# Hybrid encoder, FFN: first weights split beside the output projection's last tile, another order of the first products, down operands loaded beside the last products

## The chip, the cores and the metric

One core of one Trainium2 chip runs the whole forward pass in one launch. The metric is the device time of one execution in microseconds; the time of a kernel is the median of several runs.

## The reference, cut to what matters

Two layers over 1024 tokens of width 1024, float32 in and out. The mixer's output projection and the FFN are what the change is about:

```python
for i in range(DEPTH):                                    # DEPTH = 2
    y = mixer(x)                                          # ends in  mix @ w_out
    x = layer_norm(ALPHA * x + y, ln_mix_g[i], ln_mix_b[i])
    a, u = x @ w_gate[i], x @ w_up[i]                     # 1024 -> D_FF = 2816
    c = conv_b + sum(conv_w[j] * shifted(a, j - 1) for j in range(3))   # along the tokens
    f = (gelu(c) * u) @ w_down[i]
    x = layer_norm(ALPHA * x + f, ln_ffn_g[i], ln_ffn_b[i])
    x = x + sigmoid(x @ ple_w_gate[i]) * (p[i] @ ple_w_proj[i])
```

## The kernel before, in words

Every fp32 matrix product is made of three matmuls: an operand is split into a rounded part (h) and the rest (l), and h·h, h·l and l·h are summed in PSUM (`mm3`, lines 158 to 160). A split is a copy that rounds (on ACT by `nc.scalar.copy`, L324, or on POOL, L138) and a subtraction on DVE (`lo_part`, L141).

**Output projection** (`out_proj`, L1043 to L1077). Eight tiles of 128 tokens; each has two halves of 24 matmuls into a bank `po`, the residual addition (L1066), the LayerNorm (statistics on DVE, L869 and L872; the square root `rs` on POOL, L873 and L874; three instructions on a 128x1024 tile: `norm` L879 and times g L880 on DVE, plus b L881 on POOL, or on DVE for the last tile), the store `xmid` and, one tile later, `xt.put`: TensorE transposes the tile and the operand of the FFN is made of it.

**FFN products** (`ffn`, L1200 and on). Gate and up projections are worked in 22 blocks `m`, gate and up by turns. A block multiplies a 2 x 2 division of the weights with a 2 x 2 division of the tokens by seven products in place of eight. The weight operands are a00, a01, a11 and four sums, s1 = a10 + a11, s2 = s1 - a00, s4 = a01 - s2, s3 = a00 - a10 (`Weights`, L1079 and on; 128x512 each; tiles `wf` loaded, `ws` sums, `wh` and `wl` split parts). The token operands are made once per layer (`XSeven`, from L323): b00, b10, b11, t1 by `put`, and t2, t3, t4 in two halves by `finish` (L366 to L381), which needs the last tile: a half takes four additions on DVE or POOL (L318, 128x1024 each) and three splits. One product is 12 matmuls of 128x512. The results are summed in SBUF (`read`, L1134 to L1170): `m` copies a00 out of its bank, u = m + s2, and so on; the two banks `pa` hold a00 and s2 of a block, and the third block's a00 can't begin before the u addition of the first (L1142) has read them.

**Start.** The first two blocks (m = 0 and 1) are interleaved by hand, since the tokens' sums are still being made: a00 and a01 of both, then s1, s2, s3, a11, s4 of both. From block 2 on the order within a block is a00, s2, s3, s1, a01, a11, s4, and the next block's sums and splits are issued beside a block's products.

**Down projection** (`load` L1286, `down`). Gate times up goes to DRAM (`gated`, the spill L1198); then 22 pairs of tiles (128x1024 of `w_down` and of `gated`) are loaded as `dr`, split as `dh`, `dl` and multiplied two pairs at a time (bank `pd`); each token tile of the residual is `xn`, loaded from `xmid` (L1312).

The program is written as one stream. A framework works out the semaphores and a scheduler sets the order in each engine's queue, by its own estimate of times; each engine then works through its queue strictly in that order.

## Time and profile before

| | us |
|---|---|
| median of 3 runs | 3142.58 (3137.59 to 3142.8) |
| profiled execution | 3139.44 |
| its span, first to last instruction | 3137.6 |
| TensorE busy | 3023.3 (96% of the span) |
| VectorE, GpSimd busy | 2275.3, 1048.3 |
| mean granted TensorE clock | 0.987 |

The profiled execution took 3139.44 us, 3.1 us less than the median. The two layers have the same FFN; the stretch of layer 0 between 795 and 872 us (end of the output projection and first two blocks) recurs 1532.9 us later in layer 1, and the one at 1255 us (start of the down projection) recurs at 2788 us. Idle time in a view is put down to the engine, tile and line whose semaphore came last.

### The profile page before, as it was taken

The page shows a single profiled execution, that of the slowest core. Times are in us where ns is not written, and L with a number is a line of the kernel's source. Part 1 is how long each engine was busy: PE and PEld are TensorE (multiplying, and loading weights), DVE is VectorE, ACT ScalarE, POOL GpSimd, SP SyncE. Part 2 cuts the span into 40 slices and gives each one's busy share as a digit, 9 for nine tenths or more (in the row PEclk, how much of TensorE's full clock was granted, in tenths as well). Part 3 has the DMA queues.
Part 4 walks back from the last instruction along what each step waited for, and adds up shares of the span by engine and source line. Part 5 has one row for each costly group of instructions (what it writes and reads, how often), then busy time and mean ns, then how long its engine had stood idle before and what let it go on. Part 6 is the DMA issues. An engine that isn't in the chain of part 4 may idle for free.

```text
span 3137.6 us, 43123 instructions
## 1 busy us (share of the span) xinstructions
PE 3023.3 (96%) x15704; PEld 2590.5 (83%) x15704; DVE 2275.3 (73%) x3864; ACT 1182.2 (38%) x2502; POOL 1048.3 (33%) x1546
## 2 busy tenths in 40 slices
PE   8999999999799999999999999999888999999999
PEld 7888989888588888788889999998666888878887
DVE  6666487875887777766648777777679777767764
ACT  5555577761232222101225555555423222211111
POOL 4444534333422221101225555554333222201112
PEclk9999999999899999999999999999998999999999
DMA  3000100143122221623121100004322222244221
GB/s 119 28 28 25 31 28 8 36 131 124 67 81 81 86 84 67 226 101 108 54 68 31 35 28 28 28 18 134 103 99 68 81 81 81 81 167 141 101 74 67
DMA packets 89251, 237.52 MB, mean 76 GB/s; under 512 B 9040, under 2 KB 32720, under 8 KB 89040
## 3 DMA queue, kind: packets, MB, share of 16 engines
q1 hardware_dynamic: 89040, 234.76, 21.7%
q8 instruction: 125, 2.05, 0.3%
q14 instruction: 86, 0.70, 0.1%
HBM read 179.15 MB, written 55.57 MB: 75 GB/s over the span
## 4 chain that ended last, share of the span: by engine, by line
PE 82%; DVE 9%; DMA 3%; ACT 3%; issue 2%; POOL 2%; SPq 0%; DVEq 0%; ACTq 0%; POOLq 0%
PE pb L159 7%; PE pb L158 7%; PE pb L160 7%; PE xt L163 5%; PE pd L158 5%; PE pd L160 5%; PE pd L159 5%; PE pp L158 4%; PE pp L160 4%; PE pp L159 4%; PE s L582 3%; PE pa L158 3%; PE pa L160 2%; PE pa L159 2%; PE pg L158 2%
## 5 line engine op out<-in xcount | busy, mean ns | idle before, releaser
L158 PE MATMUL pd<-dh,dh 128*128 128x512 f32 x704 | 276.0, 392 | 8.5 <-ACT dh L324 7.5
L141 DVE TENSOR_TENSOR ptl<-xt,pth 128x512 fp32r<-128x512 f32 (+2 forms) x384 | 240.1, 652 | 57.8 <-ACT pth L397 41.3
L160 PE MATMUL pd<-dh,dl 128*128 128x512 f32 x704 | 275.1, 392 | 2.2 <-DVE dl L141 2.1
L1306 DVE TENSOR_TENSOR xn<-xn,pd 128x512 f32<-128x512 f32 x320 | 212.3, 684 | 88.5 <-PE pd L160 87.7
L159 PE MATMUL pd<-dl,dh 128*128 128x512 f32 x704 | 274.9, 391 | 0.0
L158 PE MATMUL pp<-wh,xth 128*128 128x384 f32 x768 | 266.4, 347 | 8.2 <-ACT wh L145 8.0
L159 PE MATMUL pp<-wl,xth 128*128 128x384 f32 x768 | 258.9, 337 | 1.3 <-DVE wl L148 1.3
L160 PE MATMUL pp<-wh,xtl 128*128 128x384 f32 x768 | 258.1, 336 | 0.0
L438 ACT ACTIVATE e<-s,nmx 128x1024 f32<-128x1024 f32 x192 | 214.4, 1118 | 96.6 <-DVE nmx L828 73.8
L158 PE MATMUL pb<-xt,wh 128*128 128x512 f32 x528 | 207.2, 392 | 0.0
L159 PE MATMUL pb<-xt,wh 128*128 128x512 f32 x528 | 206.9, 392 | 0.0
L160 PE MATMUL pb<-xt,wl 128*128 128x512 f32 x528 | 206.9, 392 | 0.0
L324 ACT CAST wh<-ws 128x512 fp32r<-128x512 f32 x132 | 81.7, 620 | 319.9 <-PE pb L159 261.8
L163 PE MATMUL xt<-ident,e 128*128 128x128 f32 x1440 | 194.7, 275 | 5.6 <-POOL e L731 3.0
L138 POOL TENSOR_SCALAR wh<-ws 128x512 fp32r<-128x512 f32 x44 | 29.8, 677 | 458.1 <-PE pa L159 428.8
L163 PEld LDWEIGHTS xt<-ident,e 128*128 128x128 f32 x1440 | 164.4, 141 | 18.7 <-POOL e L731 4.3
L141 DVE TENSOR_TENSOR wl<-ws,wh 128x512 fp32r<-128x512 f32 x176 | 160.8, 914 | 24.1 <-ACT wh L324 23.9
L324 ACT CAST dh<-dr 128x1024 fp32r<-128x1024 f32 x44 | 46.1, 1051 | 346.6 <-DMA dr<-gated 201.9
L138 POOL TENSOR_SCALAR dh<-dr 128x1024 fp32r<-128x1024 f32 x44 | 47.0, 1070 | 367.1 <-DMA dr<-in_w_down_dram 190.7
L158 PEld LDWEIGHTS pd<-dh,dh 128*128 128x128 f32 x704 | 132.9, 189 | 37.8 <-issue 8.3
L160 PEld LDWEIGHTS pd<-dh,dl 128*128 128x128 f32 x704 | 132.5, 188 | 32.9 <-DVE dl L141 5.3
L158 PEld LDWEIGHTS pp<-wh,xth 128*128 128x128 f32 x768 | 144.7, 189 | 13.8 <-ACT wh L145 8.9
(270 smaller groups left out, 8751.0 us busy)
## 6 DMA issues: line engine op xcount, KB each, us to landing
wf<-in_w_gate_dram SPq DMA_DIRECT2D x44, 512.0 KB, 3.2
wf<-in_w_up_dram SPq DMA_DIRECT2D x44, 512.0 KB, 4.2
gated<-c SPq DMA_DIRECT2D x44, 512.0 KB, 2.6
dr<-in_w_down_dram SPq DMA_DIRECT2D x44, 512.0 KB, 3.2
dr<-gated SPq DMA_DIRECT2D x44, 512.0 KB, 4.0
wr<-in_w_c_dram SPq DMA_DIRECT2D x32, 384.0 KB, 3.2
pes<-peo SPq DMA_DIRECT2D x64, 128.0 KB, 2.1
xmid<-xn SPq DMA_DIRECT2D x16, 512.0 KB, 2.9
```

Source lines behind the costliest of these rows:

```text
L138: nc.gpsimd.tensor_scalar(o, i, 1.0, 1.0, op0=ALU.mult, op1=ALU.mult)
L141: nc.vector.tensor_tensor(lo, src, f32(hi), op=ALU.subtract)
L158: nc.tensor.matmul(o, lhsT=lh, rhs=rh, start=start, stop=False)
L159: nc.tensor.matmul(o, lhsT=lh, rhs=rl, start=False, stop=False)
L160: nc.tensor.matmul(o, lhsT=ll, rhs=rh, start=False, stop=stop)
L163: nc.tensor.transpose(o, in_=i, identity=ident)
L324: nc.scalar.copy(h, v)
L438: nc.scalar.activation(dst, s, AF.Exp, bias=negmax, scale=1.0, accum_out=l)
L582: nc.tensor.matmul(s[:, kh * 512:kh * 512 + 512], lhsT=qt[:, hl, i, :], rhs=self.ks[kh][:, j, :], start=hl == 0, stop=hl == 1)
L1306: nc.vector.tensor_tensor(xns[t][:, sl], xns[t][:, sl], po, op=ALU.add)
```

## The change

It has three parts, the same in both layers.

1. In the output projection's last tile the weights of blocks 0 and 1 are loaded ahead of the products, and in the middle of its second half tile 6 is put and a00 and a01 of block 0 are split. The LayerNorm's last addition (plus b) of tile 6 is on DVE in place of POOL.
2. For blocks 0 and 1 all four weight sums are on POOL (s2 and s4 were on DVE), and so is the second addition of t4 in `finish`. `finish` is in two halves, whose t3 and t4 are split later. The order of the first products is a00, a01 of both blocks, then s1, s4, s2, s3, a11. The bank of s1 is freed by a copy on ACT; c00 has a tile of its own; of the additions that used the bank one is on POOL.
3. The down projection's first two pairs, the eight `xn` tiles and the next two pairs are loaded beside the seven products of the last block (`before_down`) and not behind them. To have room, the pool of split tiles stays as it was in the output projection.

On POOL, around the LayerNorm of tile 6 (`rs` ending in 10244, xn 10154) and of tile 7 (`rs` 10335 before, 10349 after), the order before was:

```order
L881 TENSOR_TENSOR xn_2415_10044<-xn_2415_10044,lngb_2353_9583 128x1024
L873 TENSOR_SCALAR rs_2448_10244<-mv_2447_10243 128x1
L874 TENSOR_TENSOR rs_2448_10244<-rs_2448_10244,mhalf_73 128x1
L881 TENSOR_TENSOR xn_2437_10154<-xn_2437_10154,lngb_2353_9583 128x1024
L318 TENSOR_TENSOR ws_2464_10358<-wf_2461_10351 128x512
L318 TENSOR_TENSOR ws_2466_10360<-wf_2460_10350,wf_2461_10351 128x512
L138 TENSOR_SCALAR wh_2470_10370<-wf_2460_10350 128x512
L873 TENSOR_SCALAR rs_2457_10335<-mv_2456_10334 128x1
L874 TENSOR_TENSOR rs_2457_10335<-rs_2457_10335,mhalf_73 128x1
L318 TENSOR_TENSOR ws_2472_10374<-wf_2463_10355 128x512
L318 TENSOR_TENSOR ws_2474_10376<-wf_2462_10354,wf_2463_10355 128x512
```

Tile 6's `rs` and plus b stood ahead of all sums. Now the same stretch of POOL reads (L874, L875 and L882 are the old L873, L874 and L881; names that begin with `w` are weights):

```order
L882 TENSOR_TENSOR xn_2415_10044<-xn_2415_10044,lngb_2353_9583 128x1024
L138 TENSOR_SCALAR w_2460_10331<-wf_2450_10256 128x512
L318 TENSOR_TENSOR ws_2464_10359<-wf_2451_10257 128x512
L318 TENSOR_TENSOR ws_2465_10360<-wf_2450_10256,wf_2451_10257 128x512
L874 TENSOR_SCALAR rs_2448_10244<-mv_2447_10243 128x1
L318 TENSOR_TENSOR ws_2464_10359<-ws_2464_10359,wf_2450_10256 128x512
L875 TENSOR_TENSOR rs_2448_10244<-rs_2448_10244,mhalf_73 128x1
L318 TENSOR_TENSOR ws_2465_10360<-wf_2450_10256,ws_2464_10359 128x512
L318 TENSOR_TENSOR ws_2468_10371<-wf_2453_10261 128x512
L318 TENSOR_TENSOR ws_2469_10372<-wf_2452_10260,wf_2453_10261 128x512
L318 TENSOR_TENSOR ws_2468_10371<-ws_2468_10371,wf_2452_10260 128x512
L318 TENSOR_TENSOR ws_2469_10372<-wf_2452_10260,ws_2468_10371 128x512
```

Eight sums now stand in a row around the second half of tile 6's `rs` and ahead of tile 7's, and tile 6's plus b is gone from here.

On DVE, up to the u addition of block 0 (`u` from `m` and `pa`; `xt2`, `xt3` and `xt4` are the token operands, `t3` and `t4` their sums), the rows before were:

```order
L141 TENSOR_TENSOR xt2_2503_10478<-t2_2430_10116,xt2_2502_10477 128x1024
L318 TENSOR_TENSOR t3_2508_10483<-t2_2430_10116,xb00_2370_9728 128x1024
L318 TENSOR_TENSOR t4_2509_10484<-xb10_2374_9732,t2_2430_10116 128x1024
L141 TENSOR_TENSOR wl_2526_10582<-wf_2463_10355,wh_2525_10581 128x512
L318 TENSOR_TENSOR t4_2509_10484<-t4_2509_10484,xb10_2376_9734 128x1024
L141 TENSOR_TENSOR wl_2529_10601<-ws_2467_10361,wh_2528_10600 128x512
L141 TENSOR_TENSOR wl_2531_10605<-ws_2475_10377,wh_2530_10604 128x512
L141 TENSOR_TENSOR xt4_2507_10482<-t4_2509_10484,xt4_2506_10481 128x1024
L141 TENSOR_TENSOR xt3_2505_10480<-t3_2508_10483,xt3_2504_10479 128x1024
L141 TENSOR_TENSOR wl_2537_10631<-wf_2514_10536,wh_2536_10630 128x512
L1142 TENSOR_TENSOR u_2527_10585<-m_2481_10403,pa_2480_10390 128x512
```

The second half's t4 and t3 splits were the last of the token operands. Now DVE has there:

```order
L141 TENSOR_TENSOR xt3_2484_10455<-c_2480_10451,xt3_2483_10454 128x1024
L141 TENSOR_TENSOR xt4_2486_10457<-c_2480_10451,xt4_2485_10456 128x1024
L141 TENSOR_TENSOR w_2505_10541<-ws_2469_10372,w_2505_10541 128x512
L141 TENSOR_TENSOR xt3_2499_10510<-t_2494_10505,xt3_2498_10509 128x1024
L141 TENSOR_TENSOR xt4_2501_10512<-t_2495_10506,xt4_2500_10511 128x1024
L141 TENSOR_TENSOR w_2508_10563<-wf_2451_10257,w_2508_10563 128x512
L141 TENSOR_TENSOR w_2509_10566<-wf_2453_10261,w_2509_10566 128x512
L141 TENSOR_TENSOR w_2527_10714<-wf_2510_10569,w_2527_10714 128x512
L141 TENSOR_TENSOR w_2520_10637<-wf_2510_10569,w_2520_10637 128x512
L318 TENSOR_TENSOR ws_2515_10602<-ws_2515_10602,wf_2510_10569 128x512
L318 TENSOR_TENSOR ws_2516_10603<-wf_2510_10569,ws_2515_10602 128x512
L1158 TENSOR_TENSOR u_2517_10608<-m_2471_10390,pa_2470_10377 128x512
```

The additions of t4's second term are gone from the row, the t3 and t4 splits of both halves stand together behind the t2 split, and the u addition still comes behind all of them.

On SP, at the end of layer 0's products (L1198 and L1236 are the spill of `gated`), the DMAs before were:

```order
L1198 DMA gated0_93<-c_2458_10345 128x1024
L1286 DMA dr_3110_13761<-in_w_down_dram 128x1024
L1286 DMA dr_3087_13715<-gated0_93 128x1024
L1198 DMA gated0_93<-c_2458_10345 128x1024
L1286 DMA dr_3113_13767<-gated0_93 128x1024
L1312 DMA xn_3090_13721<-xmid0_91 128x1024
...
L1286 DMA dr_3098_13737<-in_w_down_dram 128x1024
```

The `xn` loads followed the last spill. Now SP has there:

```order
L1236 DMA gated0_93<-c_2480_10451 128x1024 x2
L1273 DMA dr_2909_13438<-in_w_down_dram 128x1024
L1273 DMA dr_2912_13444<-gated0_93 128x1024
L1273 DMA dr_2949_13596<-in_w_down_dram 128x1024
L1273 DMA dr_2916_13464<-in_w_down_dram 128x1024
L1273 DMA dr_2919_13470<-gated0_93 128x1024
L1273 DMA dr_2952_13602<-gated0_93 128x1024
L1286 DMA xn_2924_13491<-xmid0_91 128x1024
...
L1273 DMA dr_2935_13537<-in_w_down_dram 128x1024
L1236 DMA gated0_93<-c_2480_10451 128x1024 x2
L1273 DMA dr_2938_13543<-gated0_93 128x1024
```

The four loads of the first two pairs and all eight `xn` loads now stand ahead of the last block's two spills; before, one of the four stood between the two spills and the eight behind both.

The diff, cut to its core:

```diff
-        def finish(self):
...
-            for j in range(2):
...
-                split_value(t2, h["t2"], l["t2"])
-                add(t3, t2, h["b00"], ALU.subtract)
-                add(t4, h["b10"], t2, ALU.subtract)
-                add(t3, t3, l["b00"], ALU.subtract, nc.gpsimd)
-                add(t4, t4, l["b10"])
+        def finish(self, j, temps):
+
...
+            t2, (t3, t4) = self.t2[j], temps
+            add(t3, t2, h["b00"], ALU.subtract)
+            add(t3, t3, l["b00"], ALU.subtract, nc.gpsimd)
+            add(t4, h["b10"], t2, ALU.subtract)
+            add(t4, t4, l["b10"], ALU.add, nc.gpsimd)
+            split_value(t2, h["t2"], l["t2"])
+            self.t2[j] = None
+
+            def step():
+                split_value(t3, h["t3"], l["t3"])
                 split_value(t4, h["t4"], l["t4"])
-                split_value(t3, h["t3"], l["t3"])
-            self.t2 = None
+            return step
 
...
-        def linear(t):
+        def linear(t, beside):
             mh, ml = m.pop(t)
...
                 for k in range(NK):
+                    if n == 1 and k == NK // 2:
+                        beside()
                     mm3(po, mh[:, k, :], ml[:, k, :], w[k][0][:, sl], w[k][1][:, sl], k == 0, k == NK - 1)
...
@@ -1069,10 +1072,18 @@
         for t in range(NT):
             residual(t)
             load(t + 1)
-            linear(t)
-            if t:
-                xt.put(t - 1, xns[t - 1])
-            ln(xns[t], t == NT - 1)
+            if t == NT - 1:
+                early(0)
+
+                def beside():
+                    xt.put(t - 1, xns[t - 1])
+                    early(1)
+                linear(t, beside)
+            else:
+                linear(t, lambda: None)
+                if t:
+                    xt.put(t - 1, xns[t - 1])
+            ln(xns[t], t >= NT - 2)
             nc.sync.dma_start(out=xmid[i][t], in_=xns[t])
...
-        def steps(self, make=None):
...
-                add(s3, a00, a10, ALU.subtract, nc.gpsimd)
-                add(s2, s1, a00, ALU.subtract)
-                add(s4, a01, s2, ALU.subtract)
...
+        def sums(self, eng=None):
+            (a00, a01), (a10, a11) = ((r[:, 0:4, :], r[:, 4:8, :]) for r in self.r)
+            s12, s34 = (unit("ws", [P, 2, 4, P]) for _ in range(2))
+            s1, s2, s3, s4 = s12[:, 0], s12[:, 1], s34[:, 0], s34[:, 1]
+            add(s1, a10, a11, ALU.add, nc.gpsimd)
+            add(s2, s1, a00, ALU.subtract, eng)
+            add(s4, a01, s2, ALU.subtract, eng)
+            add(s3, a00, a10, ALU.subtract, nc.gpsimd)
+            self.v.update({"a11": a11, "s1": s1, "s2": s2, "s3": s3, "s4": s4})
+
...
+        def go_ahead(self, c00):
+
+            self.ahead, self.c00 = True, c00
+            self.sums.insert(0, ("k5", ("s1",)))
...
+                elif name == "k5":
+                    self.c11 = mid2("c11", [P, 512])
+                    nc.scalar.copy(self.c11, self.o["s1"])
+                elif name == "c11" and self.ahead:
+                    nc.gpsimd.tensor_tensor(self.u2, self.u2, self.c11, op=ALU.add)
+                    nc.vector.tensor_tensor(self.c11, self.u3, self.c11, op=ALU.add)
...
+    def ffn_early(w):
+        def early(n):
+            if n == 0:
+                w[0].load()
+                w[1].load()
+            else:
+                w[0].split("a00")
+                w[0].split("a01")
+        return early
...
-        new_region(2)
-        w[0].load()
-        w[1].load()
...
-        order = [(0, "a00"), (0, "a01"), (1, "a00"), (1, "a01"), (0, "s1"), (1, "s1"), (0, "s2"), (1, "s2"), (0, "s3"), (1, "s3"),
-                 (0, "a11"), (1, "a11"), (0, "s4"), (1, "s4")]
...
-            if n == 1:
-                late()
-                for q in ("s1", "s2"):
-                    for a in range(2):
-                        steps[a][n2[q]]()
-                xt.finish()
-            if n == 4:
-                w[2].load()
-                w[3].load()
-            if n in (5, 6, 7):
...
+        def before_down(j):
+
+            if j in (0, 1):
+                load(j)
+            if j in (2, 3):
+                for t in range(4 * (j - 2), 4 * (j - 2) + 4):
+                    xns.append(unit("xn", [P, 1024]))
+                    nc.sync.dma_start(out=xns[t], in_=xmid[i][t])
+            if j in (4, 5):
+                load(j - 2)
+
+
+        pr = [Products(w[m], xt) for m in range(NF)]
+        order = [(0, "a00"), (0, "a01"), (1, "a00"), (1, "a01")]
+        order += [(m, name) for name in ("s1", "s4", "s2", "s3", "a11") for m in range(2)]
+        order += [(m, name) for m in range(2, NF) for name in Products.ORDER]
+        w[0].sums(nc.gpsimd)
+        w[1].split("a00", False)
+        w[1].split("a01", False)
+        w[1].sums(nc.gpsimd)
...
+            if n == 1:
+                c00 = unit("c00", [P, 2, 512])
+                for a in range(2):
+                    pr[a].go_ahead(c00[:, a])
+                w[0].split("s1")
+                w[1].split("s1")
+            if n == 2:
+                late()
+                new_c()
+                c2 = late_c[0]
+                first[0] = xt.finish(0, [c2[:, a, :].rearrange("p (k q) -> p k q", k=2) for a in range(2)])
+            if n == 3:
+                w[0].split("s4")
+                w[1].split("s4")
+                w[0].split("s2", True)
+                w[1].split("s2", True)
+            if n == 4:
+                first[1] = xt.finish(1, [unit("t", [P, 2, 512]) for _ in range(2)])
+            if n == 5:
+                w[0].split("s3")
+                first[0]()
+                w[1].split("s3")
+                first[1]()
+            if n == 6:
+                w[0].split("a11")
+                w[1].split("a11")
+                w[2].load()
+            if n == 7:
+                w[3].load()
+                todo = w[2].steps()
+            for _ in range({8: 1, 10: 2, 11: 1, 12: 1, 13: 3}.get(n, 0)):
+                todo.pop(0)()
...
+            if m == NF - 1:
+                before_down(Products.ORDER.index(name))
+        finished(len(order) - 1)
...
-        load(0)
-        load(1)
-        for t in range(NT):
-            xns.append(unit("xn", [P, 1024]))
-            nc.sync.dma_start(out=xns[t], in_=xmid[i][t])
-        load(2)
-        load(3)
         yield xns
```

## Rows read from the trace of the kernel before

**Rows 1.** Part 1 of the page: busy time of TensorE (PE), its weight loads, VectorE (DVE), ScalarE (ACT) and GpSimd (POOL), with the share of the span and the number of instructions.

```profile
PE 3023.3 (96%) x15704; PEld 2590.5 (83%) x15704; DVE 2275.3 (73%) x3864; ACT 1182.2 (38%) x2502; POOL 1048.3 (33%) x1546
```

**Rows 2.** The windows view, busy microseconds of each engine in a stretch with the number of instructions that began in it, then PEclk (the granted TensorE clock as a share of 2.4 GHz), the DMA share and GB/s. The first stretch lies in the middle of layer 0's products; the next two are the start of the products in layer 0 and in layer 1; the last two are slices of the start in layer 0.

```profile
1000.00:1200.00 200.00, 200.00 (x875) 163.03 (x874) 157.19 (x231) 59.79 (x86) 50.40 (x51) 1.00 0.24 85
801.00:872.00 71.00, 52.66 (x200) 40.88 (x199) 67.12 (x88) 22.92 (x36) 28.36 (x21) 0.81 0.15 52
2334.00:2405.00 71.00, 52.38 (x200) 40.66 (x198) 67.29 (x88) 23.14 (x37) 28.31 (x21) 0.81 0.15 52
835.00:850.00 15.00, 6.12 (x13) 4.08 (x14) 15.00 (x15) 3.70 (x6) 7.15 (x3) 0.61 0.31 105
850.00:865.00 15.00, 15.00 (x56) 12.01 (x56) 11.76 (x19) 3.98 (x6) 4.29 (x5) 0.82 0.01 1
```

**Rows 3.** The view of waits on PE between 780 and 880 us (layer 0's start): who waited, for which engine, tile and line, then microseconds in total, number of times, longest.

```profile
PE pa L158 <- DVE u L1142: 7.5, 1, 7.5
PE pa L158 <- ACT wh L324: 4.6, 1, 4.6
PE pa L158 <- ACT xt L324: 3.3, 1, 3.3
PE pa L160 <- DVE wl L141: 1.6, 1, 1.6
```

**Rows 4.** The same view of PE over the whole run.

```profile
PE pa L158 <- DVE u L1142: 15.2, 2, 7.7
...
PE pd L158 <- ACT dh L324: 7.5, 2, 3.9
```

**Rows 5.** The timeline of DVE in layer 0's start: begin, duration, line, operation, output tile and inputs, shapes.

```profile
794.87 0.21 DVE L872 BATCH_NORM_AGGREGATE mv<-st 128x2 f32<-128x12 f32 x1
...
822.25 0.68 DVE L141 TENSOR_TENSOR wl<-ws,wh 128x512 fp32r<-128x512 f32 x1
...
824.23 1.23 DVE L141 TENSOR_TENSOR xt<-t,xt 128x1024 fp32r<-128x1024 f32 x1
825.38 1.22 DVE L318 TENSOR_TENSOR t<-t,xb 128x1024 f32<-128x1024 f32 x1
826.51 1.22 DVE L318 TENSOR_TENSOR t<-xb,t 128x1024 f32<-128x1024 f32 x1
827.65 2.88 DVE L141 TENSOR_TENSOR wl<-ws,wh 128x512 fp32r<-128x512 f32 x1
...
839.71 2.86 DVE L141 TENSOR_TENSOR wl<-wf,wh 128x512 fp32r<-128x512 f32 x1
...
848.77 1.27 DVE L1142 TENSOR_TENSOR u<-m,pa 128x512 f32<-128x512 f32 x2
```

**Rows 6.** The timeline of POOL in the same stretch.

```profile
795.16 0.19 POOL L873 TENSOR_SCALAR rs<-mv 128x1 f32<-128x1 f32 x1 [6.22 <-DVE mv L872]
...
798.36 2.39 POOL L881 TENSOR_TENSOR xn<-xn,lngb 128x1024 f32<-128x1024 f32 x1 [2.37 <-DVE xn L880]
801.10 1.28 POOL L318 TENSOR_TENSOR ws<-wf 128x512 f32<-128x512 f32 x1 [0.34 <-PE po L160]
...
823.08 0.62 POOL L138 TENSOR_SCALAR wh<-ws 128x512 fp32r<-128x512 f32 x1 [8.83 <-DVE wl L141]
826.68 3.30 POOL L318 TENSOR_TENSOR t<-t,xb 128x1024 f32<-128x1024 f32 x1 [2.98 <-DVE t L318]
...
838.74 3.29 POOL L318 TENSOR_TENSOR t<-t,xb 128x1024 f32<-128x1024 f32 x1 [5.16 <-DVE t L318]
```

**Rows 7.** The groups of POOL instructions by line and shape between 794.9 and 848.8 us: count, busy microseconds, mean ns of one, idle time before them and its releaser.

```profile
L318 POOL TENSOR_TENSOR t<-t,xb 128x1024 f32<-128x1024 f32 x2 | 6.6, 3296 | 8.1 <-DVE t L318 8.1
L318 POOL TENSOR_TENSOR ws<-wf,wf 128x512 f32<-128x512 f32 x3 | 5.0, 1660 | 0.0
...
L138 POOL TENSOR_SCALAR wh<-wf 128x512 fp32r<-128x512 f32 x4 | 4.4, 1118 | 0.0
```

**Rows 8.** The windows view again: the first 45 us of the down projection in layer 0, the 45 us behind them, and the first 45 us in layer 1.

```profile
1255.00:1300.00 45.00, 39.35 (x162) 30.71 (x161) 30.96 (x38) 5.19 (x6) 5.22 (x5) 0.96 0.70 266
1300.00:1345.00 45.00, 45.00 (x200) 37.26 (x200) 36.77 (x48) 7.33 (x7) 6.33 (x6) 1.00 0.47 164
2787.70:2832.70 45.00, 39.95 (x163) 30.91 (x162) 30.54 (x39) 5.47 (x6) 5.24 (x5) 0.96 0.70 267
```

**Rows 9.** The view of waits on PE between 1255 and 1300 us.

```profile
PE pd L158 <- ACT dh L324: 3.9, 1, 3.9
PE pd L160 <- DVE dl L141: 1.3, 1, 1.3
```

**Rows 10.** The timeline of SP's DMA queue at the end of layer 0's products (the time is that of the issue).

```profile
1229.69 0.32 SPq L1286 DMA_DIRECT2D dr<-gated  x1
1237.02 0.33 SPq L1286 DMA_DIRECT2D dr<-in_w_down_dram  x1
...
1255.22 0.33 SPq L1286 DMA_DIRECT2D dr<-in_w_down_dram  x1
1255.60 0.45 SPq L1286 DMA_DIRECT2D dr<-gated  x1
```

**Rows 11.** The timeline of ACT there.

```profile
1241.75 1.03 ACT L324 CAST dh<-dr 128x1024 fp32r<-128x1024 f32 x1
1260.54 1.04 ACT L324 CAST dh<-dr 128x1024 fp32r<-128x1024 f32 x1 [17.77 <-DMA dr<-gated]
```

More of the change, by code (lines that the diff above doesn't have):

```diff
@@ L1163, in read @@
                 elif name == "c00":
-                    plus(self.m, self.m, "a01")
-                    self.c00 = self.m
+                    if self.c00 is None:
+                        self.c00 = self.m
+                    plus(self.c00, self.m, "a01")
                 elif name == "c10":
```

116 lines of the change are left out of this document (45 added, 71 removed).

## Prediction

> **What bounds the kernel now.** I read the page's busy times first: TensorE is busy 96% of the span, the other engines are far below [rows 1]. The windows say where the last 4% are: in the middle of the products PE has 875 matmuls in 200 us and no idle time, which is 0.2286 us for each [rows 2]. So nothing in the steady blocks can be gained, and what the change does there (other buffers, the same instructions) I put at nothing: PE covers it, and DVE has 43 us of slack in 200. The places that the change touches are two in each layer. At the start of the products 200 matmuls begin in 71 us [rows 2] where 71/0.2286 = 310 would fit: 25 us are lost per layer. In the first 45 us of the down projection 162 begin where the next 45 us hold 200: 38 x 0.225 = 8.6 us lost, and 37 x 0.225 = 8.3 in layer 1 [rows 8]. Together 67 us are the most that both layers could give back. The view of waits names them: at the start 7.5 us for the u addition on DVE, 4.6 and 3.3 for casts on ACT, 1.6 for a split on DVE [rows 3], in both layers alike (15.2 us, two times [rows 4]); at the down projection 3.9 for a cast of a loaded operand and 1.3 for its split [rows 9]. Behind the u addition stands DVE: between 835 and 850 us it is busy for 15.00 of 15.00 us while PE has 6.12 [rows 2]. So the start is a question of DVE's queue up to that addition, not of PE.
>
> **What holds DVE.** Its prices: 0.60 us from start to start for a 128x512 instruction in SBUF (duration 0.68), 1.14 for 128x1024 (824.23, 825.38, 826.51) [rows 5]. POOL's: 1.28 for a 128x512 sum, 2.39 for a 128x1024 addition, 0.62 for a copy [rows 6]. But the 128x512 split that costs 0.68 alone took 2.88 and 2.86 while POOL did an addition of 128x1024, and that addition took 3.30 and 3.29 in place of 2.39 [rows 5, 6]. The split ends at 827.65 + 2.88 = 830.53, POOL's addition at 829.98; the other pair at 842.57 and 842.03. So DVE waited for POOL to the end and then worked its own 0.55 us, and POOL had waited for the DVE instruction before it. The Trainium skill, page "SBUF — State Buffer", section "Who interferes with whom", has this as a rule: of a DVE instruction with two SBUF inputs and a GpSimd one that reads SBUF the later is blocked until the first is done; the trace agrees in these four rows. I take from the rows that work in SBUF on the two engines adds up, save where DVE reads PSUM or is idle.
>
> **The start, step by step.** From tile 6's aggregate (794.87) to the end of the two u additions (848.77 + 1.2) [rows 5] are 55.0 us of DVE. By the order these are 19 instructions of 128x512 (11.4 us), 15 of 128x1024 (17.1), 20 of 128x256 at 0.33 (6.6), two norms, the statistics and a residual addition (4.0): 39.1 of its own. In the same time POOL has five sums (6.4), three 128x1024 additions (7.2) and six copies (about 4): 17.8. Stepping both queues in their order, the later of two SBUF instructions waiting for the other, DVE is held for 12.2 us and idle for 3.8, and the u addition comes at 850.2, within 1 us of the trace; without the holding it would be 13 us too early. That is why I trust the stepping for the new order, estimate as it is.
> The change takes four sums and one t4 addition for each half off DVE, and gives it tile 6's plus b, two c00 additions and an earlier split: 16 of 128x512 and 14 of 128x1024, 36.7 us in all. POOL gets nine sums, four 128x1024 additions and eight copies: 26.2. DVE gains 2.4 and is held for 20.7 in place of 12.2, with 4.4 idle: 61.8 us, 6.8 more. It also begins later: tile 6's `rs`, which POOL did at 795.16, straight after the aggregate [rows 6], stands behind two sums and is cut by a third, and plus b follows on DVE; the tile, whose plus b ended at 800.75, is ready at about 806.8, and the row starts 1.9 us later. The u addition so comes 8.7 us later, at 858.2 us. The Trainium skill, page "Perfetto Trace Analysis", section "Optimizing Scalar/DVE Operations", says that offloading between these two engines "might not help", as they share a port; on this part it speaks against the change. By the rows it is so here: DVE loses 8.5 - 2.4 = 6.1 us net by the move. (Where it were not so, the sum would be that of rival 1.)
> What pays is the order of the products. Before, PE could do 8 of the 14 first products (a00, a01, s1, s2) ahead of the u addition, now 12 (s4 and s3 too): 4 x 12 x 0.2268 = 10.9 us of matmuls are moved into the wait. PE's own gaps in the new order: it begins a00 at 807.7 in place of 806.5, a gap of 6.3 us ahead of s2's second half, which needs t2 of the second half, and 4.3 us ahead of the third block. Net 10.9 - 8.7 = 2.2, and with less of it at the lower granted clock (0.61 and 0.82 in the slices before [rows 2]) 3.1 us. In layer 1 another sum stands ahead of the power in `rs`, and the same steps give 1.7. Bounds per layer: with POOL's additions 1.25 times as long the start gives back up to 5 us less than that, so about -2; without any holding it gives 9 us more.
> The early split of a00 and a01 of block 0 takes the 4.6 us wait for ACT's cast [rows 3] away, but only in name: tile 6's transposes, which stand in front of these products on PE, are now late themselves, by 6 us. The copy of s1's bank on ACT is free, ACT is busy 22.92 of 71 us [rows 2]; POOL's one addition on u falls behind the critical point.
>
> **The down projection.** The second pair's `dr` was issued at 1255.22 and 1255.60, when PE had begun the first pair, and ACT cast it at 1260.54 after 17.77 us of waiting for the DMA; the first pair had been loaded at 1229.69 and 1237.02 and cast at 1241.75 [rows 10, 11]. The scheduler thus had half of the gain already. Now both pairs and the `xn` loads are ahead of the last two spills, beside the seven products of the last block (84 x 0.2268 = 19 us). The 3.9 and the 1.3 go [rows 9], and most of the slow matmuls that follow them (0.96 granted [rows 8]). What is late next is DVE: the pairs' splits are four of 128x1024 (4.6 us) in the last block, and the casts of the second group behind it; I leave 0.6 us of waiting at the second group. Stepped through, the stretch from the first `pd` takes 44.2 in place of 50.4 us: 6.2 per layer, with 5.2 (the two waits alone) and 8.6 as bounds. The new spill and loads on SP stall nobody: the spill waits behind loads whose buffers are free by then, and its data are needed in the last group.
>
> **Sum.** Layer 0: 3.1 + 6.2 = 9.3; layer 1: 1.7 + 6.2 = 7.9; together 17 us off 3139.4, so 3122 by the profiled execution, which stands 3.1 under the median: 3125.
>
> **Rivals.** (1) POOL's extra work doesn't hold DVE, since it falls where DVE waits anyway: then only DVE's shorter queue counts, and the same steps give 18.6 and 13.5 us per layer with the down part, 32 in all: 3110. For it: POOL is busy only 28.36 of 71 us [rows 2]. Against it: the four stretched rows, and 12.2 us of holding without which the old order can't be had.
> (2) POOL becomes the bound of the start, and the kernel slower. The place is POOL's queue from tile 6's `rs` to the last t4 addition, where eight sums stand ahead of tile 7's `rs` and four 128x1024 additions ahead of the splits. If each of its instructions costs what it cost beside a busy DVE, 1.66, 3.30 and 1.12 [rows 7], it has 9 x 1.66 + 4 x 3.30 + 8 x 1.12 = 37.1 us, and if none of it overlaps DVE's 36.7 the row takes 73.8: the u addition comes 20.7 us later, not 8.7, and each start loses 9.6 us where 2.4 was won on average. With 12.4 from the down parts that is 6.8 us slower: 3149. It decides from a delay of about 20 us; between 15 and 20 it eats just what the down part gives, about 3140. Against it: for the old order this sum gives 39.1 + 8.3 + 9.9 + 6.7 = 64 where the trace has 55.0.
> (3) The down loads gain nothing, because the waits only move to the splits on DVE or to the second group: then only the start's 4.8 are left, 3138, no change to be measured. Against it: DVE is busy 157 of 200 us in the blocks [rows 2], so there is room for 4.6 us.
>
> **How the numbers follow.** Forecast 0.55 (3115 to 3134: gains of 9 to 25 us, from POOL 1.25 times dearer to half of the holding gone); rival 1 0.20; rival 2 slower 0.10, eating the gain 0.08; rival 3 0.07. A measurement of this kernel can tell 0.2%, 6.3 us, from no change. Faster by more than that 0.75, within it 0.15, slower 0.10. The range goes from 3107 (rival 1 with 3 us to spare) to 3139 (rival 3 within), and leaves out about 0.2: rival 2 whole, and a little past rival 1.
>
> **What would show it.** Right: PE's wait for the u addition at the third block shrinks from 7.5 to about 4, a new wait of some 6 us at s2 for the t2 operand appears; tile 6's transposes begin at about 807; DVE still has no idle time between 835 and 850; the wait for `dh` at the down projection (7.5 us in two [rows 4]) is gone, and the first 45 us there hold some 190 matmuls. Rival 1: no wait at the third block, and 128x512 splits near 0.7 us beside POOL's additions. Rival 2: POOL busy throughout the start, PE waiting for token operands t3 or t4 for over 10 us. Wrong altogether: a wait in the steady blocks (fewer than 875 matmuls in 200 us), which I put at nothing.

## The result

The changed kernel takes 3123.38 us (median of 4 runs, 3122.67 to 3124.18), the kernel before 3141.32 (4 runs): a ratio of 0.995, 95% interval 0.9937 to 0.9962. The profiled execution spans 3120.8 us where that of before spanned 3137.6, 16.8 us less. Page part 1 of the changed kernel:

```profile
PE 3014.5 (97%) x15704; PEld 2589.3 (83%) x15704; DVE 2295.5 (74%) x3850; ACT 1184.5 (38%) x2506; POOL 1084.9 (35%) x1560
```

Against [rows 1] PE has the same 15704 instructions and is busy 9 us less; DVE is busy 20 us longer and POOL 37, though DVE has 14 instructions fewer and POOL 14 more. Both helpers work longer, and the kernel is faster all the same.

To see where, I take the time at which the same matmul begins in both traces, counting matmuls. "Start" goes from the output projection's last tile (the 337th `po` matmul of layer 0; in layer 1 the 317th, 20 earlier, which makes both numbers there 5.8 us longer) to the 1001st matmul of the layer's products; "blocks" from there to the last product matmul; "down" from there to the 601st `pd` matmul.

| us | before | changed | difference | predicted |
|---|---|---|---|---|
| start, layer 0 | 270.74 | 267.62 | -3.1 | -3.1 |
| start, layer 1 | 276.41 | 275.85 | -0.6 | -1.7 |
| blocks, both layers | 388.33 | 387.78 | -0.6 | 0 |
| down, layer 0 | 144.82 | 137.87 | -6.95 | -6.2 |
| down, layer 1 | 144.52 | 137.58 | -6.94 | -6.2 |
| all else (unchanged code) | 1912.7 | 1914.1 | +1.4 | 0 |

The last line isn't put down to the change: in the traces of all the runs below, the stretch between the layers alone varies between 917.4 and 922.6 us with the same code. Kernels with the same start differ too: the changed kernel, e2_start_only and e9_region below by up to 0.5 us in layer 0 and 0.9 in layer 1. So the 0.6 us of layer 1 can't be told from nothing.

The windows of the changed kernel (busy microseconds with counts, then granted clock, DMA share, GB/s):

```profile
801.00:872.00 71.00, 55.26 (x218) 44.18 (x219) 69.42 (x78) 22.52 (x35) 44.10 (x26) 0.88 0.13 45
...
835.00:850.00 15.00, 10.51 (x42) 7.76 (x41) 15.00 (x9) 4.94 (x6) 12.11 (x6) 0.94 0.30 103
1000.00:1200.00 200.00, 200.00 (x875) 162.96 (x874) 163.06 (x232) 60.12 (x87) 52.87 (x50) 1.00 0.23 82
1251.20:1296.20 45.00, 43.81 (x193) 35.68 (x192) 34.75 (x44) 6.21 (x6) 6.28 (x6) 1.00 0.67 237
2777.10:2822.10 45.00, 43.98 (x195) 36.03 (x194) 34.80 (x45) 6.22 (x6) 6.29 (x6) 1.00 0.68 240
```

At the start 218 matmuls begin in 71 us where 200 did, and in the slice from 835 to 850 us 42 where 13 did [rows 2]; DVE is busy for 15.00 of 15.00 us in it as before, and POOL for 12.11 where it was 7.15. The middle of the blocks has its 875 matmuls in 200 us still. The first 45 us of the down projection hold 193 and 195, not 162 and 163 [rows 8].

PE's waits at the start of layer 0, to set beside [rows 3]:

```profile
PE xt L163 <- DVE xn L882: 8.5, 2, 6.1
PE pb L159 <- DVE xt L141: 3.8, 1, 3.8
PE pa L158 <- DVE u L1158: 3.1, 1, 3.1
...
PE pa L159 <- DVE xt L141: 0.7, 1, 0.7
```

and two of layer 1:

```profile
PE xt L163 <- DVE xn L882: 10.9, 2, 5.5
PE pa L158 <- DVE u L1158: 4.4, 1, 4.4
```

The 7.5 us for the u addition have become 3.1 and 4.4. In place of the 4.6 for ACT's cast PE now waits for tile 6's and tile 7's LayerNorm, 8.5 and 10.9 us in two waits, and the second half of a token operand has a wait of 3.8 (it is s3's, `pb`, not s2's). DVE's timeline (begin, duration), to set beside [rows 5]:

```profile
800.51 1.74 DVE L880 TENSOR_SCALAR xn<-xn,mv,rs 128x1024 f32<-128x1024 f32 x1 [4.15 <-POOL rs L875]
...
804.49 2.17 DVE L882 TENSOR_TENSOR xn<-xn,lngb 128x1024 f32<-128x1024 f32 x1
...
835.38 3.41 DVE L141 TENSOR_TENSOR xt<-t,xt 128x1024 fp32r<-128x1024 f32 x1
...
839.73 6.75 DVE L141 TENSOR_TENSOR xt<-c,xt 128x1024 fp32r<-128x1024 f32 x2
...
856.42 1.28 DVE L1158 TENSOR_TENSOR u<-m,pa 128x512 f32<-128x512 f32 x2
```

and POOL's, to set beside [rows 6]:

```profile
799.92 0.55 POOL L875 TENSOR_TENSOR rs<-rs,mhalf 128x1 f32<-128x1 f32 x1
...
825.80 4.66 POOL L138 TENSOR_SCALAR w<-ws 128x512 fp32r<-128x512 f32 x1 [6.64 <-PE pb L160]
...
831.00 6.70 POOL L318 TENSOR_TENSOR c<-c,xb 128x1024 f32<-128x1024 f32 x2
...
839.24 6.16 POOL L318 TENSOR_TENSOR t<-t,xb 128x1024 f32<-128x1024 f32 x2
```

Tile 6's `rs`, whose power ends at 800.47, is done 4.3 us behind the beginning of the aggregate (796.16); before, it was done 1.1 us behind it (at 795.99). DVE stands idle for 4.15 us until then; the norm takes 1.74 and plus b 2.17, beside POOL's sums. Of the token operands' splits of 128x1024 one costs 3.41 and two cost 6.75, where one alone costs 1.14, while POOL does its additions. The u addition begins at 856.42, that is 66.9 us behind the beginning of this stretch (789.52); before, 58.9 behind it (848.77 and 789.84), so it is 8.0 us later. In layer 1 it is 9.7 later (68.6 us behind the beginning, 58.9 before).

### The profile page after: what moved, and what is told of

Its sections match the earlier page's. It is cut to its first block, busy times and chain, and to the rows that moved or that the text cites. A ratio compares the mean times of both kernels' runs of the same rounds, so it can differ in the third digit from the quotient of the medians.

```text
span 3120.8 us, 43023 instructions
## 1 busy us (share of the span) xinstructions
PE 3014.5 (97%) x15704; PEld 2589.3 (83%) x15704; DVE 2295.5 (74%) x3850; ACT 1184.5 (38%) x2506; POOL 1084.9 (35%) x1560
## 4 chain that ended last, share of the span: by engine, by line
PE 60%; DVE 5%; DMA 2%; POOL 2%; issue 1%; ACT 1%; SPq 0%; DVEq 0%; ACTq 0%; POOLq 0%
PE pb L160 5%; PE pb L159 5%; PE pb L158 5%; PE pd L158 5%; PE pd L159 5%; PE pd L160 5%; PE s L583 4%; PE pp L159 3%; PE pp L160 3%; PE pp L158 3%; PE pa L158 2%; PE xt L163 2%; PE pa L160 2%; PE pa L159 2%; PE pg L158 2%; PE pg L160 2%
## 5 line engine op out<-in xcount | busy, mean ns | idle before, releaser
L324 ACT CAST w<-ws 128x512 fp32r<-128x512 f32 x132 | 81.5, 621 | 355.7 <-PE pb L160 284.1
L159 PE MATMUL pb<-xt,w 128*128 128x512 f32 x528 | 207.2, 392 | 7.2 <-DVE xt L141 7.2
L158 PE MATMUL pb<-xt,w 128*128 128x512 f32 x528 | 206.8, 392 | 0.0
L160 PE MATMUL pb<-xt,w 128*128 128x512 f32 x528 | 206.4, 391 | 0.0
L138 POOL TENSOR_SCALAR w<-ws 128x512 fp32r<-128x512 f32 x44 | 34.9, 794 | 426.5 <-PE pa L160 403.2
L141 DVE TENSOR_TENSOR w<-ws,w 128x512 fp32r<-128x512 f32 x176 | 160.5, 914 | 1.5 <-ACT w L324 0.5
L160 PEld LDWEIGHTS pd<-dh,dl 128*128 128x128 f32 x704 | 132.1, 188 | 27.6
```

The costliest lines, as they stand in the source:

```text
L138: nc.gpsimd.tensor_scalar(o, i, 1.0, 1.0, op0=ALU.mult, op1=ALU.mult)
L141: nc.vector.tensor_tensor(lo, src, f32(hi), op=ALU.subtract)
L158: nc.tensor.matmul(o, lhsT=lh, rhs=rh, start=start, stop=False)
L159: nc.tensor.matmul(o, lhsT=lh, rhs=rl, start=False, stop=False)
L160: nc.tensor.matmul(o, lhsT=ll, rhs=rh, start=False, stop=stop)
L324: nc.scalar.copy(h, v)
```

## Experiments

Ten kernels ran; each is judged by its time and by the stretches of the table above, read in its trace. Ratios go by the kernel before as it ran beside each: 3138.93 us with e1 to e5, 3140.99 with e6 to e9, 3140.08 with e10 and e11.

| us | start 0 | start 1 | blocks 0 | down 0 | down 1 | median |
|---|---|---|---|---|---|---|
| before | 270.74 | 276.41 | 194.17 | 144.82 | 144.52 | 3138.9 to 3141.3 |
| changed | 267.62 | 275.85 | 193.86 | 137.87 | 137.58 | 3123.38 |
| e1_down_only | 270.60 | 275.97 | 194.77 | 136.23 | 136.23 | 3122.68 |
| e2_start_only | 268.09 | 276.71 | 194.11 | 142.34 | 142.22 | 3133.54 |
| e4_t4_dve | 266.15 | 274.57 | 193.89 | 138.73 | 138.09 | 3121.15 |
| e5_no_pool | 259.67 | 264.21 | 193.91 | 138.95 | 138.86 | 3103.87 |
| e6_old_order | 271.93 | 281.04 | 193.89 | 139.58 | 137.32 | 3131.40 |
| e7_before_no_pool | 267.61 | 273.99 | 194.25 | 145.28 | 145.34 | 3133.39 |
| e8_ahead | 256.56 | 263.02 | 193.89 | 138.78 | 137.22 | 3101.95 |
| e9_region | 268.09 | 276.04 | 194.68 | 137.00 | 137.02 | 3125.45 |
| e10_copies_act | 265.59 | 272.77 | 193.91 | 138.35 | 137.43 | 3119.84 |
| e11_sums_dve | 269.92 | 275.57 | 193.88 | 138.87 | 139.04 | 3126.30 |

**The parts apart.** The down part alone, put on the kernel before (`before_down` and `load` as in the change, ahead of the product loop):

```diff
+            if m == NF - 1:
+                before_down(Products.ORDER.index(name))
         finished(len(order) - 1)
...
-        load(0)
-        load(1)
...
         yield xns
```

> The kernel before with part 3 alone: the first two pairs, the xn tiles and the next two pairs of the down projection are loaded beside the last block's seven products; the start of the products is as before. Theory (the two parts are independent, and the down part is the larger): the stretch from the last product to the 200th matmul of the down projection loses 6.9 us per layer, as in the changed kernel, so about 13.9 us in all, 3127.5 where the kernel before has 3141.3; the start keeps its 7.5 us wait for the u addition. Rival (the down part needs the room that the changed start leaves in the buffers, or lives on the changed pool of split tiles): under 7 us in all, 3135 or more.

Measured 3122.68 us (3121.37 to 3124.27), ratio 0.9948, interval 0.9936 to 0.9961: as much as the whole change within the intervals, so parts 1 and 2 add nothing to part 3 that the time shows. The start is as before, with a wait of 7.7 us for the u addition. The down stretch loses 8.6 and 8.3 us, more than the 6.9 expected and all of the loss that the windows had shown, and the blocks ahead of it are 0.6 us longer. The window of its first 45 us is as full as any:

```profile
1252.90:1297.90 45.00, 45.00 (x201) 37.24 (x200) 36.39 (x47) 6.27 (x7) 6.57 (x6) 1.00 0.56 197
```

The changed kernel with this part undone:

```diff
-            if m == NF - 1:
-                before_down(Products.ORDER.index(name))
         finished(len(order) - 1)
+        for j in range(6):
+            before_down(j)
```

> The changed kernel with part 3 undone: the down operands and xn tiles are issued behind the last product again. Theory: only the start's gain is left, 3.4 us in layer 0 and 0.6 in layer 1 by the trace of the changed kernel, about 4 in all: 3137, no change that can be measured; the down projection has its wait of some 3.9 us for a cast of dh again. Rival (the start alone is worth the larger part, by the page's 0.995): 3130 or less.

Measured 3133.54 us (3130.28 to 3136.43), ratio 0.9982, interval 0.9973 to 0.9991: 5.4 us, between the theory and the rival, of which the starts have 2.6 and -0.3 and the down stretches 2.5 and 2.3. PE's waits at the down projection there:

```profile
PE pd L158 <- ACT dh L324: 2.1, 1, 2.1
PE pd L160 <- DVE dl L141: 0.7, 2, 0.6
```

The wait for `dh` is 2.1, not 3.9 [rows 9], with the loads behind the last product again. So a third of the changed kernel's down gain comes from elsewhere than `before_down`; the pool of split tiles that now stays open is what is left of the change at that place, but it wasn't run alone.

**Does POOL's work hold DVE?** Four runs move work between the two. In the first, the second addition of t4 goes back to DVE:

```diff
-            add(t4, t4, l["b10"], ALU.add, nc.gpsimd)
+            add(t4, t4, l["b10"])
```

> The changed kernel with the second addition of t4 back on DVE (two of 128x1024 per layer), all else as changed. Theory (work in SBUF on POOL and DVE adds up): POOL loses 2 x 2.39 us, DVE gains 2 x 1.14, so the u addition comes some 2.5 us earlier and the start ends 3.0 us earlier per layer: about 3118. Rival (POOL's work runs beside DVE's, so each instruction taken from DVE helps): the u addition comes 2.1 us later, the start ends 0.6 us later per layer: about 3125.

Measured 3121.15 us (3118.06 to 3122.12); the starts end 1.5 and 1.3 us earlier than in the changed kernel. In these stretches the sign is the theory's and the size half of it; the time itself can't show it (17.8 us under the kernel before, 17.9 with the change). Then everything off POOL, also what was there before the change: s1, s3, t3's addition and the copies (the start of `split` and the addition of c11 to u are changed likewise):

```diff
-            add(t3, t3, l["b00"], ALU.subtract, nc.gpsimd)
+            add(t3, t3, l["b00"], ALU.subtract)
-            add(t4, t4, l["b10"], ALU.add, nc.gpsimd)
+            add(t4, t4, l["b10"])
...
-        w[0].sums(nc.gpsimd)
+        w[0].sums(nc.vector, nc.vector)
```

> The changed kernel with nothing of the first two blocks left on POOL but the LayerNorm's rs: all four weight sums, both second additions of t3 and t4 and the addition of c11 to u are on DVE, the rounding copies of a01, a11 and s3 of these two blocks on ACT. Theory (work in SBUF on the two engines adds up, and POOL takes twice as long for it): the splits beside it cost 0.68 again, tile 6's transposes begin before 802 us, the u addition comes at about 846.7 in place of 856.4 and the start ends 11 us earlier per layer, so about 3101. Rival (they run side by side): DVE has some 13 instructions more to do and nothing in return, the u addition comes 3.7 us later than without the holding, and the start ends 3.6 us later per layer than in the changed kernel: about 3130.

Measured 3103.87 us (3102.6 to 3105.85), ratio 0.9889, interval 0.9876 to 0.9903. The starts end 8.0 and 11.6 us earlier than in the changed kernel. DVE has more to do and is done earlier:

```profile
834.55 0.69 DVE L141 TENSOR_TENSOR w<-ws,w 128x512 fp32r<-128x512 f32 x1
835.15 2.35 DVE L141 TENSOR_TENSOR xt<-c,xt 128x1024 fp32r<-128x1024 f32 x2
837.42 0.68 DVE L141 TENSOR_TENSOR w<-ws,w 128x512 fp32r<-128x512 f32 x1
838.02 2.35 DVE L141 TENSOR_TENSOR xt<-t,xt 128x1024 fp32r<-128x1024 f32 x2
...
842.09 3.42 DVE L141 TENSOR_TENSOR w<-wf,w 128x512 fp32r<-128x512 f32 x2 [0.51 <-POOL w L138]
...
847.46 1.27 DVE L1159 TENSOR_TENSOR u<-m,pa 128x512 f32<-128x512 f32 x2
```

The splits of 128x1024 are at 2.35 for two, where two took 6.75, those of 128x512 at 0.68; the u addition begins at 847.46, 58.8 us behind the beginning of the stretch, 8.1 earlier than in the changed kernel. Only at 842.09, where POOL makes the third block's copies and sums, do two splits take 3.42 again. PE's waits:

```profile
PE pa L158 <- DVE u L1159: 5.8, 1, 5.8
PE xt L163 <- DVE xn L882: 2.4, 1, 2.4
```

The wait for the LayerNorm falls from 8.5 to 2.4; that for the u addition is 5.8, since PE comes to it earlier than DVE does. The rival, which gave 3130, is out. The same on the kernel before, with its old order and late down loads:

```diff
+            g = None if make else nc.gpsimd
...
-                add(s1, a10, a11, ALU.add, nc.gpsimd)
-                add(s3, a00, a10, ALU.subtract, nc.gpsimd)
+                add(s1, a10, a11, ALU.add, g)
+                add(s3, a00, a10, ALU.subtract, g)
```

> The kernel before with nothing of the first two blocks' operands on POOL but LayerNorm: the sums s1 and s3 and t3's second addition on DVE, the copies of a01, a11 and s3 of these blocks on ACT; order of the products, and the down projection, as before. Theory (POOL's work in SBUF holds DVE for 12.2 us of the row up to the u addition): DVE has five sums' and two additions' worth of instructions more, and still the u addition comes about 4 us earlier and the start ends 3.9 us earlier per layer: 3131. Rival (they run side by side): DVE's own work grows by 5 to 6 us, the start ends some 6 us later per layer: 3151.

Measured 3133.39 us (3130.83 to 3135.28), ratio 0.9974, interval 0.9963 to 0.9986; the starts end 3.1 and 2.4 us earlier than before (3.9 expected, 6 later by the rival). t3's addition ran on DVE with the rest. Its u addition begins at 844.91, 56.5 us behind the stretch's beginning, 2.4 earlier than before. PE still waits there, and 5.6 us for a split that is now later:

```profile
PE pa L158 <- DVE u L1143: 6.5, 1, 6.5
PE pa L160 <- DVE wl L141: 5.6, 1, 5.6
```

Last, the copies and the sums by themselves:

```diff
-            split_value(self.v[name], hl[:, 0], hl[:, 1], nc.gpsimd if name in self.HI else None)
+            split_value(self.v[name], hl[:, 0], hl[:, 1], nc.gpsimd if name in hi else None)
```

with `hi` empty for the first two blocks:

> The changed kernel with the rounding copies of a01, a11 and s3 of the first two blocks on ACT and not on POOL (six of 128x512 per layer); POOL's sums and additions as changed. Theory (POOL's copies, with one input in SBUF, hold DVE as its additions do): the u addition comes 3 us earlier and the start ends 2.7 us earlier per layer, 3118. Rival (copies don't hold DVE, and the splits' second halves only wait longer for ACT's queue): the start ends up to 2.9 us later per layer, 3123 to 3129.

Measured 3119.84 us (3115.35 to 3123.99); the starts end 2.0 and 3.1 us earlier than in the changed kernel, and the u addition begins 64.25 us behind the stretch's beginning, 2.7 earlier:

```profile
853.07 1.28 DVE L1159 TENSOR_TENSOR u<-m,pa 128x512 f32<-128x512 f32 x2
```

DVE's idle time up to there is the same in both (5.1 and 5.2 us), so its instructions got shorter: copies on POOL, with one input, hold DVE too. For the sums `w[0].sums(nc.gpsimd)` and `w[1].sums(nc.gpsimd)` became `w[0].sums()` and `w[1].sums()`:

> The changed kernel with s2 and s4 of the first two blocks back on DVE (four sums of 128x512 per layer). Theory (work on the two engines adds up; a sum costs DVE 0.60 for POOL's 1.28, but these sums fall where DVE is partly idle, waiting for tile 6's LayerNorm): tile 6's transposes begin 0.7 us earlier, the start ends within 0.3 us of the changed kernel's: 3123. Rival (each POOL sum taken away is worth its whole difference, 4 x 0.68 us): 2.7 us earlier per layer, 3118.

Measured 3126.30 us (3124.31 to 3128.42); the start of layer 0 ends 2.3 us later, that of layer 1 0.3 earlier. The rival's 2.7 us earlier are out; the theory's "within 0.3" holds for layer 1 alone. The 2.3 us of layer 0 stand in the trace: tile 6's transposes began 0.35 us earlier, counted from the stretch's beginning, but two of POOL's copies (826.72 and 832.53) took 5.84 and 4.64 us beside DVE's instructions. So t3's additions on POOL began only at 837.14, ACT cast their result at 839.57, and DVE was idle for 3.96 us until then. In layer 1 one copy took 5.83, the next 0.61, and DVE had no such gap.

DVE's row of each trace can be taken apart in the same way, as an estimate. Its instructions have a usual step from one to the next when nothing disturbs them, 0.60 us for 128x512, 1.14 for 128x1024, 0.33 for 128x256; the sum of these is called own work here, what the steps took beyond that is called held. In layer 0, from the stretch's beginning to the u addition (0.2 to 0.3 us of it lie ahead of the first instruction):

| us | own | held | idle | all |
|---|---|---|---|---|
| before | 43.2 | 11.1 | 4.4 | 58.9 |
| changed | 43.0 | 18.4 | 5.2 | 66.9 |
| e4_t4_dve | 45.3 | 14.0 | 5.5 | 65.2 |
| e5_no_pool | 52.0 | 3.6 | 3.0 | 58.8 |
| e7_before_no_pool | 47.9 | 2.1 | 6.3 | 56.5 |
| e10_copies_act | 42.7 | 16.3 | 5.1 | 64.3 |
| e11_sums_dve | 45.4 | 13.2 | 9.0 | 67.9 |

With each piece of POOL's work that leaves the stretch the held time falls, also where DVE's own work grows. In e5_no_pool tile 6's transposes begin 6.1 us earlier as well, which could have been the cause; in DVE's row it is worth 2.1 us of idle time, the held time 14.8. In e7_before_no_pool they begin when they did before.

**What is the order worth?** The changed kernel with the old order of the first products:

```diff
-        order += [(m, name) for name in ("s1", "s4", "s2", "s3", "a11") for m in range(2)]
+        order += [(m, name) for name in ("s1", "s2", "s3", "a11", "s4") for m in range(2)]
```

> The changed kernel with the first products in the order of before, s1, s2, s3, a11, s4 behind a00 and a01; engines, buffers and part 3 as changed. Theory of the prediction (the new order is worth 4 x 12 x 0.2268 = 10.9 us per layer, since four more products stand ahead of the u addition): the start ends about 11 us later per layer, 3145. Milder theory (with the old order the u addition itself comes earlier, since s2's operands are made first; stepping the queues gives the u addition 6 us earlier and the end of the start 4.7 us later): about 3133. Rival (the order is worth nothing): 3123.

Measured 3131.40 us (3128.34 to 3137.05), ratio 0.9972, interval 0.9962 to 0.9982; the starts end 4.3 and 5.2 us later than in the changed kernel. The u addition of block 0 begins at 852.17 there, 61.5 us behind the stretch's beginning and 5.4 earlier than in the changed kernel, and PE waits for other things:

```profile
PE xt L163 <- DVE xn L882: 8.5, 2, 6.1
PE pb L158 <- POOL w L138: 3.1, 1, 3.1
PE pa L159 <- DVE xt L141: 2.8, 1, 2.8
PE pb L160 <- DVE w L141: 2.3, 1, 2.3
```

The milder theory's number (4.7 per layer) holds; 10.9 is out. Its reason, that s2's operands are made first, isn't in the rows: DVE does the same instructions in both kernels up to the splits of a11. Behind these the changed kernel has two splits and two sums of the third block's weights (from wf_2510 in the order above) ahead of the u addition, stretched by POOL's sums of that block (849.85 and 851.47):

```profile
849.69 5.08 DVE L141 TENSOR_TENSOR w<-wf,w 128x512 fp32r<-128x512 f32 x4
854.69 1.09 DVE L318 TENSOR_TENSOR ws<-ws,wf 128x512 f32<-128x512 f32 x1
855.81 0.69 DVE L318 TENSOR_TENSOR ws<-wf,ws 128x512 f32<-128x512 f32 x1
```

With the old order it stands right behind the splits of a11:

```profile
850.97 1.28 DVE L141 TENSOR_TENSOR w<-wf,w 128x512 fp32r<-128x512 f32 x2
852.17 0.68 DVE L1158 TENSOR_TENSOR u<-m,pa 128x512 f32<-128x512 f32 x1
```

From the first of these splits to the u addition are 6.7 us there and 1.2 here, which is the 5.4. And the starts are 1.2 and 4.6 us longer than in the kernel before: part 1 and the moves to POOL cost that much together, and the order makes up for it.

**The down part's remainder.** In the changed kernel SP's queue (time of issue, duration) reads:

```profile
1235.83 10.48 SPq L1273 DMA_DIRECT2D dr<-gated  x2
1246.41 4.20 SPq L1286 DMA_DIRECT2D xn<-xmid  x8
1250.82 0.33 SPq L1273 DMA_DIRECT2D dr<-in_w_down_dram  x1
1252.73 1.73 SPq L1236 DMA_DIRECT2D gated<-c  x2
```

Two loads of `gated` take 10.48 us to be issued, the second for a third-group tile whose buffer PE still reads, and the eight `xn` loads stand behind them. A pool of its own takes that load away from there:

```diff
         finished(len(order) - 1)
+
+        new_region(4)
```

> The changed kernel with a new pool of split tiles opened behind the last product, as the kernel before had it, so that the third group's loads can't be issued ahead of the xn loads. In the changed kernel SP stood for 10.5 us at a load of gated for the third group, which waits for a buffer of the last block's a01, with the eight xn loads behind it; the down part alone, put on the kernel before, where this does not occur, gave 8.6 us per layer and not 6.9. Theory (this wait on SP costs the difference): the down stretch shrinks by 1.6 us per layer, and about 3 us in all, 3120.5. Rival (the difference has to do with the start, or with where the DMAs fall): 3123 as it was.

Measured 3125.45 us (3121.03 to 3126.31), ratio 0.9947: no gain. The down stretch does shrink by 0.9 and 0.6 us, but the blocks ahead are 0.8 us longer in each layer, and PE has a wait there, between 1205 and 1250 us, that the changed kernel has not:

```profile
PE pa L158 <- ACT m L1168: 0.6, 1, 0.6
```

ACT's copy of `m` comes later because DVE is held once more: POOL's rounding copy of the second pair's `w_down`, which the changed kernel makes at 1239.58, now falls beside one of DVE's convolution steps, which takes 1.53 us where it takes 0.74 in the changed kernel:

```profile
1231.41 1.43 POOL L138 TENSOR_SCALAR dh<-dr 128x1024 fp32r<-128x1024 f32 x1 [4.21 <-DVE w L141]
1231.85 1.53 DVE L1227 SCALAR_TENSOR_TENSOR c<-c,convt,c 128x511 f32<-128x511 f32 x1
```

The addition on u that ACT waits for ahead of that copy comes 0.8 us later by it. e1_down_only has the same pair at 1232.51, the same wait, 0.5 us, and the same growth of the blocks. So what is won by freeing SP is lost in the last block.

**A better version.** e5_no_pool with the bank of s2 freed by ACT and the third block's sums issued one product later:

```diff
-                    plus(self.u2, self.m, "s2")
+                    if self.ahead:
+                        nc.scalar.copy(self.u2, self.o["s2"])
+                        nc.vector.tensor_tensor(self.u2, self.m, self.u2, op=ALU.add)
+                    else:
+                        plus(self.u2, self.m, "s2")
...
-            for _ in range({8: 1, 10: 2, 11: 1, 12: 1, 13: 3}.get(n, 0)):
+            for _ in range({9: 1, 11: 2, 12: 2, 13: 3}.get(n, 0)):
```

> The kernel without POOL in the first two blocks (the experiment that ran at 3103.87), and in addition the bank of s2 is freed by a copy on ACT, as that of s1 is, with the addition of m then in SBUF, and the third block's sums are issued one product later. Theory (what is left of the start's wait, 5.8 us at the third block, is DVE's row up to the reading of s2's bank): the wait shrinks to about 3 us and the start ends 3 us earlier per layer, 3098. Rival (DVE's row is as long as before, and what is not waited for here is waited for at the next bank): no change, 3104.

Measured 3101.95 us (3097.31 to 3102.49), ratio 0.9873, interval 0.986 to 0.9887. The starts end 3.1 and 1.2 us earlier than in e5_no_pool, and the time is 1.9 us shorter, 4 if each is taken against the kernel before beside it, not 6. PE's wait is now for a split:

```profile
PE pa L160 <- DVE w L141: 3.1, 2, 2.7
...
PE pb L158 <- DVE u L1159: 1.6, 1, 1.6
```

It is the fastest version of this study, 39 us under the kernel before. Its interval overlaps that of e5_no_pool.

## Why the prediction was right, and where it was not

- **What bounds the kernel** held: what changed are the start and the down projection, and the blocks kept 875 matmuls in 200 us.
- **Work of the two engines adds up** held, and it is the step that made the forecast; without it the sum would have been rival 1's, 3110. The stepping gave 12.2 us of holding before and 20.7 after, the rows give 11.1 and 18.4. e5_no_pool and e7_before_no_pool take POOL's work away and DVE, with more instructions, is done sooner; e10_copies_act shows it for copies. The size for t4's addition (e4_t4_dve) was half of the 3.0 us.
- **Tile 6's LayerNorm** was forecast ready at 806.8; PE began its transposes at 806.80. It is a cost of DVE's row too, which is idle for 4.15 us there; the idle time up to the u addition is 5.2 us in all, where the prediction had 4.4.
- **The u addition** was forecast at 858.2 us, which by the sum is nearer the end of the two additions than their beginning; they began at 856.42 and ended at 857.70. The wait at the third block, forecast 4.3, was 3.1 and 4.4. The forecast wait of 6.3 us at s2's second half was 0.7 there and 3.8 at s3's: PE got t2 sooner and t3 later; in sum the waits are 7.6 where 10.6 were forecast.
- **Net of the start**: 3.1 in layer 0 as forecast; 0.6, not 1.7, in layer 1, where the u addition came 9.7 us later and tile 7's LayerNorm kept PE waiting over 5 us, a wait that the text did not have. The 3.1 is in part luck: it is the difference of two terms, and both were put too high.
- **"What pays is the order: 10.9 us"** is the step that failed, inside a right sum. e6_old_order gives 4.3 and 5.2. The prediction set all of the u addition's delay (8.7, measured 8.0) against the engine moves, but 5.4 us of it go when the old order is put back: with s2 later among the products, the u addition stands behind the third block's splits and sums on DVE. So the order is worth about 5, and without it part 1 and the moves would have made the starts 1.2 and 4.6 us longer than before.
- **The down projection** was mis-sized by 0.75 us per layer: 6.95 and 6.94 for 6.2. The waits for `dh` and its split went as stated, PE waits 1.2 and 1.0 us for the residual addition in their place, and the first 45 us hold 193 matmuls, for "some 190". Of the gain 2.5 and 2.3 us remain without the early loads (e2_start_only), and the early loads alone, on the kernel before, give 8.6 and 8.3 and cost 0.6 in the blocks. The prediction added the two parts; they overlap: with part 3 alone the time is that of the whole change, so the start's 4.8 us of the sum aren't seen in it.
- **Rival 2** (POOL as the bound, slower) had the right place and not the price: the u addition came 8.0 us later, not 20.7. **Rival 3** (the down loads gain nothing) is out by e1_down_only.
- **Two readings were wrong**, without weight in the sum. The load issued at 1255.22 belongs to the third group, as dr_3110 in the order on SP; the second pair's loads are those of 1237.02 and 1255.60, the first pair's were issued at 1219.07 and 1229.69, so three of the four loads were early already. The 17.77 us ahead of the cast at 1260.54 are ACT's idle time; the load that ended them had been issued 4.9 us before. And 3115, the low end of the range, stands 27.6 us under the median, not 25.

## What to carry to other kernels

When work on SBUF by a second engine stretches that of the busy one, as POOL's does DVE's here, count the two together: step both queues up to the instruction that PE waits for, and move work to the engine that needs less time for it, or to a third engine (here ACT, which took six copies per layer and so made the starts 2.0 and 3.1 us shorter). By the estimate above DVE was held for six to seven tenths of the time that POOL's work there takes alone (11.1 of 17.8 us, 18.4 of 26.2, the second figures from the prediction). A moved instruction pays only if it leaves that sum smaller; here taking all of POOL's work off the first two blocks, the change's moves and what was there before, was worth 17 to 20 us, as much as the change. And price a reordering with all queues stepped: an addition whose product comes later can fall behind other work in its engine's queue, here 5.4 us of it.

## What was not expected of the hardware

POOL can lose for long, not only for one instruction. Its copy of 128x512 at 825.80, 0.62 us by itself, took 4.66 us, while DVE ran five instructions on SBUF data one behind the other:

```profile
825.29 1.21 DVE L318 TENSOR_TENSOR c<-t,xb 128x1024 f32<-128x1024 f32 x1
826.42 1.21 DVE L318 TENSOR_TENSOR c<-xb,t 128x1024 f32<-128x1024 f32 x1
827.56 1.21 DVE L141 TENSOR_TENSOR xt<-t,xt 128x1024 fp32r<-128x1024 f32 x1
828.69 1.28 DVE L141 TENSOR_TENSOR w<-ws,w 128x512 fp32r<-128x512 f32 x2
829.90 0.67 DVE L1158 TENSOR_TENSOR c<-m,pb 128x512 f32<-128x512 f32 x1
```

Only when DVE turned to a sum out of PSUM, at 829.90, was the copy done, at 830.46. The two additions at 831.00 then took 6.70 us where two alone take 4.8, and DVE's instructions beside them were stretched likewise.
